# A planner's timeline model for the first half of a transformer layer, and a pool of its own for attention's queries and keys

## The chip, the cores and the metric

The kernel runs on one core of one Trainium2 chip. A core has a matrix engine (TensorE, PE in the profile, with its weight loads as PEld), a vector engine (VectorE, DVE), a scalar engine (ScalarE, ACT), a third elementwise engine (GpSimd, POOL) and SyncE (SP), which here only issues transfers. Each engine works through its own queue of instructions in order; semaphores make one engine wait for another. The metric is the device time of one execution in microseconds, as the median of several runs.

## The reference

One layer of an encoder on 1024 tokens of width 1024, in float32:

```
x = x + 1/2 * post1(SwiGLU_1(pre1(x)))                # first FFN, inner width 2816
u = pre_mix(x)
[ret_q|ret_k|ret_v|ret_g|na_q|na_k|na_v|g_ret|g_na] = u @ W_mix_in
y_ret = W_ret_out(silu(ret_g) * headnorm(retention forward + backward))   # 4 heads
y_na  = W_na_out(2-D neighbourhood attention(na_q, na_k, na_v) + bias)    # 8 heads
x = x + post_mix(W_mix_out(sigmoid(g_ret) * y_ret + sigmoid(g_na) * y_na))
x = x + 1/2 * post2(SwiGLU_2(pre2(x)))                # second FFN
```

pre, post and headnorm are RMS norms; ret_q and ret_k are rotated by position (rotary) before the retention.

## The kernel before

**Precision.** Each float32 operand is split into a high part and a low part (`split`, lines 60 and 61: ACT casts the high part, DVE, or POOL where told, subtracts it from the source for the low part). A product is three matmuls, high by high, low by high and high by low (`mm3`, lines 87 to 89). So a 128x512 piece of weights costs one transfer, one ACT cast, one DVE subtraction and then matmuls.

**Stages.** In order: the first norm and its transposes (`norm_T`, `flip`, line 126 on PE); the first FFN's input half (`ffn_in`, `Pairs.run`), its output half (`ffn_out`) with an epilogue that squares, scales and normalises (`Epilogue`: L525 on ACT, L526 on POOL, L97 the reciprocal root on POOL, L536 and L547 on DVE); the mixing pairs; attention (`na_cores`) and retention (`ret_cores`), with other projections filled in between; the mixing output; the second FFN.

**Pairs.** The wide projections use Winograd's form of a 2x2 block product with seven products in place of eight. One call of `Pairs.run` is one job: it loads two 128x1024 pieces (raw, tag `wraw`, 4 buffers), makes differences of them in place on DVE (L383, L384, L397, L408), splits them (tags `wh`, `wl`, 9 buffers each) and evicts the seven products from PSUM (L381 on ACT, L387 to L414 on DVE). The mixing stage has 14 jobs: four for attention's queries and keys, then four rotary jobs alternating with four silu jobs, then two sigmoid jobs. A rotary job calls `rotate` for each of its four parts (L866 to L869), on POOL and DVE in turn. The results (attention's queries `nq` and keys `nk`, the gates `sn`, and so on) are stored to memory by POOL's queue (`store`, line 67) and read back later.

**Order.** The kernel is written in program order, but the framework's scheduler orders the instructions of every queue when it plans the program: it keeps program order as a priority, simulates the engines with a model of their costs, and at each simulated moment queues the ready instruction of the highest priority. On the chip each queue then runs in that fixed order. Three devices steer it: `Filler` interleaves pieces of independent work (an n in FILL tuples is a number of such steps), `high_priority` lifts a few instructions, and `behind` or `issue_after` put one instruction after another.

**Where the halves meet.** After the last sigmoid job the pools of the first half are closed (`left.close()`), the pool `mix` is opened, and `na_cores` starts. It loads head pair 0's keys (`load(0)`, as a `wraw` tile) and queries (`qload(0)`, four transfers, L699), splits them (L60/L61 and L63/L64), then runs `fill(n0)`, 12 steps of the value projection of the retention (`vproj(wrv...)`: one step is one `mm3`, three matmuls; three steps use up one 128x512 piece of weights), and then the first scores (L744). PSUM has eight banks: six of tag `ps`, two of tag `pt`. All tiles of `na_cores` come from one pool, `na`, whose memory lies over that of the closed pools of the first half.

Of the kernel before, what the change touches and what calls it, by code (L numbers as in the profile page):

```python
# [26 lines left out]
RH = 4  # L27
NHP = 4

NA_FILL = (12, 2, 2)  # L30
RET_FILL = (14, 2, 2, 4, 2, 3, 0, 1, 2)
FLIP_FILL = (8, 8, 8, 8, 2)
NA_UNITS = ((0, 0, 0), (3, 1, 0), (1, 0, 1), (1, 0, 2), (4, 1, 1), (4, 1, 2), (2, 0, 3), (5, 1, 3))
# [651 lines left out]
    return lhs  # L685


def na_cores(c, pool, d, bias, fill, n0, n1, n2, side={}):


    nc = c.nc
# [1 line left out]

    def qload(hp):

        qraw[hp] = [pool.tile([P, S], F32, tag="qraw", name="qraw", bufs=2) for _ in range(2)]
        for e in range(2):
            for half in range(2):
                nc.sync.dma_start(qraw[hp][e][64 * half:64 * half + 64], d["nq"][hp][64 * e:64 * e + 64])  # L699

    def qsplit(hp, cb):

        qop[hp, cb] = []
        for e in range(2):
            q = [pool.tile([P, 16, 16], F32R, tag=f"q{e}{p}", name=f"q{p}", bufs=2) for p in "hl"]
            c.split(*q, qraw[hp][e].rearrange("p (r c) -> p r c", c=64)[:, :, 16 * cb:16 * cb + 16], scale=0.125)
            qop[hp, cb].append([p.rearrange("p r c -> p (r c)") for p in q])

    def load(hp):
        if hp == 0:  # L710
            kr = c.raw(d["nk"][hp])
        else:
            kr = pool.tile([P, S], F32, tag="kraw", name="kraw", bufs=1)
            nc.sync.dma_start(kr, d["nk"][hp])

        kop[hp] = [pool.tile([P, S], F32R, tag=f"k{e}", name=f"k{e}", bufs=2) for e in range(2)]
        for e in range(2):
            es, es_ = slice(64 * e, 64 * e + 64), slice(64 - 64 * e, 128 - 64 * e)
            for b in range(2):
# [310 lines left out]
def trunk_layer(ctx: ExitStack, tc, x, g1a, w1i, w1o, g1b, gma, wmt, wnv, wrv, logits, dtab, rope, bias,  # L1030
# [26 lines left out]
    def rows(a):  # L1057
        return lambda t: a[t * P:(t + 1) * P, :]
# [4 lines left out]
        return stack.enter_context(tc.tile_pool(name=name, bufs=1, side=side))  # L1063


    apool = pool(right, "a1", "right")
    early = pool(right, "early", "right")
    wx = Winograd(c, (apool,) * 3, early, (14,) * 7)
    with tc.tile_pool(name="norm1", bufs=1) as ep:
        g = ep.tile([P, D], F32, tag="gpre", name="gpre", bufs=1)  # L1070
        nc.sync.dma_start(g, g1a)
        for t in range(TT):
            xt = ep.tile([P, D], F32, tag="epx", name="epx", bufs=3)
            nc.sync.dma_start(xt, x[t * P:(t + 1) * P, :])
            f = c.norm_T(xt, g, t, ep, wx.put)()
            if f is not None:
                f()
        fin = Pairs(c, wx, [(w1i[i], w1i[FT + i]) for i in LeftFactors.order], 3, 3)
        fin.lead(lambda: early.tile([P, 512], F32, tag="lead", name="lead", bufs=6), on_pool=(3, 4, 5, 0))
    g0 = pool(left, "gl10")  # L1080
    with tc.tile_pool(name="fin1", bufs=1) as fp:
        fin.side = Filler(right_factors(c, fin, early, "lead", 6, w1o, wf[0], 35))
        ffn_in(c, fin, fp, LeftFactors(c, early, gl[0]))
    right.close()

    spool = pool(left, "s1")
    x0pool = pool(right, "x0", "right")
    x1_stack = ExitStack()
    x1pool = pool(x1_stack, "x1", "right")
    wx = Winograd(c, (x0pool, x1pool, spool), None, (4, 4, 2, 8, 8, 8, 8), d["a21"])  # L1090
    ep_stack, g_stack = ExitStack(), ExitStack()
    ep = pool(ep_stack, "ep1")
    g1 = pool(g_stack, "gl11")
    xt = [x1pool.tile([P, 4, 512], F32, tag="x", name="x", bufs=2) for _ in range(2)]
    xt += [spool.tile([P, 4, 512], F32, tag="x", name="x", bufs=8) for _ in range(2)]
    junk = spool.tile([P, 4, 512], F32, tag="x", name="junk", bufs=8)
    q = [p.tile([P, 4, 512], F32, tag="x", name="q", bufs=n) for p, n in ((ep, 2), (ep, 2), (spool, 8), (spool, 8))]
    ahead = {}
    fo = Epilogue(c, ep, g1b, gma, rows(x), rows(x1), wx.put)
    rest = ffn_out(c, xt, [junk[:, i] for i in range(4)], q, Blocks(c, (g0, g1, g1, g1), (1, 3)), w1o, wf[0], gl[0], fo,  # L1100
                   {n: (lambda j=j: ahead.update({j: c.load_w(wnv[j])})) for j, n in enumerate((65, 66, 73))})
    g_stack.close()
    wx.tmp = pool(g_stack, "cmb1")


    a21 = []

    def xh(t, k):

        return a21 if (t, k) == (1, 0) else wx.op(("a11", "a12", None, "a22")[2 * t + k])  # L1110

    def vproj(src, groups, done):

        for toks in groups:
            banks = {t: c.bank() for t in toks}
            for k in range(KT):
                if k % 2 == 0:
                    w = ahead.pop(k // 2) if k // 2 in ahead else c.load_w(src[k // 2])
                for t in toks:
                    tt = slice((t % 4) * P, (t % 4 + 1) * P)  # L1120
                    c.mm3(banks[t], [q[:, k % 4, tt] for q in xh(t // 4, k // 4)], w[k % 2], k == 0, k == KT - 1)
                    yield
            for t in toks:
                done(t, banks[t])

    evpool = []

    def ev():
        return evpool[0].tile([P, S], F32, tag="ev", name="ev", bufs=3)

    def done_nv(t, b):
        e = evpool[0].tile([P, 512], F32, tag="ev", name="ev", bufs=6 if len(evpool) == 1 else 4)
        nc.scalar.copy(e, b)
        c.store(d["nv"][2 * t:2 * t + 2].rearrange("r c d -> (r c) d"), e)

    def done_rv(j):
        def f(t, b):
            e = ev()
            nc.scalar.copy(e[:, :512], b)
            c.store(d["rv"][t][:, j * 512:(j + 1) * 512], e[:, :512])  # L1140
        return f


    jobs = [(16 + i, 20 + i, d["nq"][i], d["nk"][i], None) for i in range(NHP)]
    for i in range(RH):
        jobs += [(i, 4 + i, d["rq"][i], d["rk"][i], "rotary"),
                 (8 + 2 * i, 9 + 2 * i, d["rg"][2 * i], d["rg"][2 * i + 1], AF.Silu)]
    jobs += [(32 + 2 * i, 33 + 2 * i, d["sn"][2 * i], d["sn"][2 * i + 1], AF.Sigmoid) for i in range(2)]
    mx = Pairs(c, wx, [(wmt[j[0]], wmt[j[1]]) for j in jobs], 3)

    def first():
        yield from vproj(wnv, ((0, 1, 2, 3),), done_nv)
        yield from mx.leads()

    fill = Filler(first())
    evpool[:] = [wx.tmp, None]
    for f, k in zip(rest, FLIP_FILL):
        fill(k)
        f = f()
        if f is not None:  # L1160
            fill(FLIP_FILL[4])
            f()
    g_stack.close()
    ep_stack.close()
    with tc.tile_pool(name="pa", bufs=1) as pa:
        evpool[:] = [pa]
        fill.drain()
        turners = (nc.gpsimd, nc.vector, nc.gpsimd, nc.vector)

        def half():  # L1170
            return pa.tile([P, 512], F32, tag="ev", name="ev", bufs=6)

        tabs = [[pa.tile([P, 512], F32, tag="tab", name="tab", bufs=4) for _ in range(2)] for _ in range(2)]
        for h in range(2):
            for j in range(2):
                nc.sync.dma_start(tabs[h][j], rope[:, j, h * 512:(h + 1) * 512])

        for i, (_, _, f, g, fn) in enumerate(jobs):
            parts = {}

            def part(j):
                parts[j] = half()
                return parts[j]

            def done(j):
                h = j % 2
                if fn == "rotary":
                    rotate(turners[j], half(), parts[j], *tabs[h])
                elif fn is not None:
                    nc.scalar.activation(parts[j], parts[j], fn)  # L1190
                c.store((f, g)[j // 2][:, h * 512:(h + 1) * 512], parts[j])
            mx.run(i, part, done)
            if i == 2:
                x1pool = pool(x1_stack, "x1b", "right")
                a21[:] = [x1pool.tile([P, 4, 512], F32R, name=f"a21{q}") for q in "hl"]
                for k in range(2):
                    raw = c.raw(d["a21"][:, 2 * k:2 * k + 2].rearrange("p k t -> p (k t)"))
                    c.split(*[q[:, 2 * k:2 * k + 2].rearrange("p k t -> p (k t)") for q in a21], raw)
            if i == NHP - 1:
                for _ in vproj(wnv, ((4, 5, 6, 7),), done_nv):  # L1200
                    pass
                for cb in range(4):
                    nc.sync.dma_start(d["nvg"][cb].rearrange("t (r c) d -> (t r) c d", r=4),
                                      d["nv"][:, KEY_OFF[cb]:KEY_OFF[cb] + 32, :])
    left.close()

    m_stack, o_stack = ExitStack(), ExitStack()
    mix = pool(m_stack, "mix")
# [49 lines left out]

    fill = Filler(products())
    dec = []  # L1260
    with tc.tile_pool(name="na", bufs=1) as na:
        na_cores(c, na, d, bias, fill, *NA_FILL, {24: lambda: dec.append(Decays(c, mix, logits, dtab))})
    dec = dec[0]
    fill.until("rv")
    with tc.tile_pool(name="ret", bufs=1) as ret:
# [155 lines left out]
```

## Time and profile before

| | us |
|---|---|
| median of 3 runs | 2291.7 (2291.03 to 2295.29) |
| the profiled execution's own time | 2290.08 |
| its span, first to last instruction | 2288.3 |
| PE busy | 2215.6 |
| DVE busy | 1700.4 |
| ACT busy | 1002.6 |
| POOL busy | 577.6 |

The span leaves 1.8 us of the execution outside it. A row in order of time has its start in us, its duration in us, engine, line, operation and `output<-inputs`, a count, and in brackets how long the engine stood idle before it and what ended that. A row of a stretch has, for each engine, busy time and the number of instructions, then the clock that PE was granted (1.00 is full speed), the busy share of the DMA engines and GB/s. Matmuls overlap, so a busy PE isn't PE at its peak; the number of PE instructions in a stretch tells more.

### The profile page before, as it was taken

To read this page: it belongs to the slowest core of one execution; us is meant where nothing else is said; L and a number is where in the kernel's file an instruction comes from. 1 tells how busy PE (TensorE), PEld (TensorE's weight loads), DVE (VectorE), ACT (ScalarE), POOL (GpSimd) and SP (SyncE) were. 2 spreads that over 40 slices of the span, in tenths; PEclk is the share of its full clock that TensorE was granted. 3 is DMA by queue.
4 is the path that set the end of the run, shared out by engine and by line. 5 is a ranking of instruction groups with operands and counts; after the bars stand their busy time and mean duration, and the time that the engine had idled before them with its cause. 6 is when DMAs were issued, how large, how long until landed. Compare 5 with 4: busy or idle time off the path is not lost.

```text
span 2288.3 us, 30130 instructions
## 1 busy us (share of the span) xinstructions
PE 2215.6 (97%) x10288; PEld 1836.6 (80%) x10288; DVE 1700.4 (74%) x2939; ACT 1002.6 (44%) x2102; POOL 577.6 (25%) x749
## 2 busy tenths in 40 slices
PE   6999999999999999999999999999899999999998
PEld 5888888878777887777888888888688888887886
DVE  8897878755878766968885677646997787875576
ACT  6332222344554222248885675315643222234453
POOL 3143434210221133411101222101324343421022
PEclk9999999999999999999999999999999999999999
DMA  4355545586653542257655467766534556447664
GB/s 156 117 189 172 189 166 193 174 279 196 228 163 138 175 162 98 94 192 249 209 175 173 157 222 237 259 228 216 189 126 156 189 175 203 155 167 244 191 234 155
DMA packets 161882, 422.62 MB, mean 185 GB/s; under 512 B 19712, under 2 KB 47488, under 8 KB 161664
## 3 DMA queue, kind: packets, MB, share of 16 engines
q1 hardware_dynamic: 121248, 286.97, 38.8%
q0 software_dynamic: 40480, 133.72, 15.7%
q8 instruction: 81, 1.33, 0.2%
q14 instruction: 73, 0.60, 0.1%
HBM read 301.60 MB, written 123.21 MB: 186 GB/s over the span
## 4 chain that ended last, share of the span: by engine, by line
PE 85%; DVE 8%; issue 2%; ACT 1%; POOL 1%; DMA 1%; POOLq 0%; DVEq 0%; SPq 0%; ACTq 0%
PE ps L89 26%; PE ps L87 26%; PE ps L88 26%; PE pt L87 1%; PE pt L88 1%; PE pt L89 1%; DVE wl L61 1%; PE ps L744 1%; PE pt L763 1%; POOL rstd L97 1%; PE pt L126 1%; DVE x L536 1%; DVE tmp L117 1%; DVE t L384 0%; PE pt L966 0%
## 5 line engine op out<-in xcount | busy, mean ns | idle before, releaser
L61 DVE TENSOR_TENSOR wl<-wraw,wh 128x512 fp32r<-128x512 f32 x662 | 500.9, 777 | 93.6 <-ACT wh L60 91.8
L60 ACT CAST wh<-wraw 128x512 fp32r<-128x512 f32 x670 | 391.0, 618 | 233.4 <-PE ps L88 82.8
L87 PE MATMUL ps<-wh,gh 128*128 128x512 f32 x612 | 239.3, 394 | 5.1 <-ACT gh L60 2.2
L88 PE MATMUL ps<-wl,gh 128*128 128x512 f32 x612 | 239.1, 392 | 3.6 <-DVE wl L61 3.6
L61 DVE TENSOR_TENSOR gl<-graw,gh 128x512 fp32r<-128x512 f32 (+2 forms) x178 | 124.0, 698 | 155.1 <-ACT gh L60 155.1
L89 PE MATMUL ps<-wh,gl 128*128 128x512 f32 x612 | 238.4, 393 | 0.9 <-DVE gl L61 0.8
L60 ACT CAST gh<-graw 128x512 fp32r<-128x512 f32 (+2 forms) x178 | 106.7, 601 | 211.2 <-PE ps L88 84.1
L60 ACT CAST wh<-t 128x512 fp32r<-128x512 f32 x58 | 36.1, 622 | 238.6 <-DVE t L384 238.6
L87 PEld LDWEIGHTS ps<-wh,gh 128*128 128x128 f32 x612 | 115.6, 189 | 30.8 <-ACT gh L60 2.6
L88 PEld LDWEIGHTS ps<-wl,gh 128*128 128x128 f32 x612 | 115.4, 189 | 29.3 <-DVE wl L61 6.1
L89 PEld LDWEIGHTS ps<-wh,gl 128*128 128x128 f32 x612 | 115.5, 189 | 25.9 <-DVE gl L61 2.0
L526 POOL TENSOR_TENSOR q<-q,gain 128x512 f32<-128x512 f32 x30 | 46.1, 1554 | 336.6 <-ACT junk L525 241.1
L89 PE MATMUL ps<-a11h,wl 128*128 128x512 f32 x280 | 112.4, 401 | 12.0 <-DVE wl L61 12.0
L87 PE MATMUL ps<-a11h,wh 128*128 128x512 f32 x280 | 113.1, 404 | 1.8 <-ACT wh L60 1.2
L88 PE MATMUL ps<-a11l,wh 128*128 128x512 f32 x280 | 111.6, 399 | 0.0
L89 PE MATMUL ps<-a12h,wl 128*128 128x512 f32 x280 | 109.6, 391 | 1.3 <-DVE wl L61 1.3
L87 PE MATMUL ps<-a12h,wh 128*128 128x512 f32 x280 | 110.6, 395 | 0.1
L87 PE MATMUL ps<-a22h,wh 128*128 128x512 f32 x280 | 109.8, 392 | 0.0
L88 PE MATMUL ps<-a12l,wh 128*128 128x512 f32 x280 | 109.3, 390 | 0.0
L89 PE MATMUL ps<-a22h,wl 128*128 128x512 f32 x280 | 109.1, 390 | 0.0
L88 PE MATMUL ps<-a22l,wh 128*128 128x512 f32 x280 | 109.1, 390 | 0.0
L400 DVE TENSOR_TENSOR c<-ps,gt 128x512 f32<-128x512 f32 x44 | 30.4, 691 | 99.5 <-PE ps L89 99.1
(362 smaller groups left out, 5967.1 us busy)
## 6 DMA issues: line engine op xcount, KB each, us to landing
wraw<-in_dram SPq DMA_DIRECT2D x243, 512.0 KB, 4.4
g0s<-cmb POOLq DMA_DIRECT2D x44, 256.0 KB, 2.7
lead<-in_dram POOLq DMA_DIRECT2D x44, 256.0 KB, 3.8
graw<-g0s SPq DMA_DIRECT2D x44, 256.0 KB, 2.8
wq<-in_dram POOLq DMA_DIRECT2D x44, 256.0 KB, 3.9
g1s<-cmb POOLq DMA_DIRECT2D x44, 256.0 KB, 3.7
graw<-g1s SPq DMA_DIRECT2D x44, 256.0 KB, 2.7
bt<-in_dram SPq DMA_DIRECT2D x24, 384.0 KB, 4.1
```

The lines of the kernel that those rows point to most:

```text
L60: nc.scalar.copy(h, src)
L61: (eng or nc.vector).tensor_tensor(l, src, hf, ALU.subtract)
L87: mm(ps, a[0], b[0], start=start, stop=False, skip_group_check=more)
L88: mm(ps, a[0], b[1], start=False, stop=False, skip_group_check=more)
L89: mm(ps, a[1], b[0], start=False, stop=stop, skip_group_check=more)
L97: self.nc.gpsimd.tensor_tensor(r[:, :n], ms, self.mhalf[:, :n], ALU.pow)
L117: nc.vector.scalar_tensor_tensor(xn[:, bs], x[:, bs], r[:, 0:1], gain[:, bs], op0=ALU.mult, op1=ALU.mult)
L126: self.nc.tensor.transpose(pt[:, j * P:(j + 1) * P], h[:, j * P:(j + 1) * P], self.ident)
L400: self.last = self.read = tt(c21, p7, c12, ALU.add).ins
L526: (eng or c.nc.gpsimd).tensor_tensor(h if out is None else out, h, self.post[:, b * 512:(b + 1) * 512], ALU.mult)
L536: nc.vector.scalar_tensor_tensor(x[:, bs], h, r[:, 0:1], x[:, bs], op0=ALU.mult, op1=ALU.add)
L744: nc.tensor.matmul(bv, q[:, rg * P:(rg + 1) * P], k, start=n == 0, stop=n == 1)
```

## The change

Everything from the first norm to the last mixing pair is put into a block of its own, `tc.block(schedule_with_timeline_sim=True)`. Inside it the scheduler plans with its second, more detailed model of the engines (TimelineSim); the rest of the kernel is planned with the default (CoreSim). By the framework's description the default leaves out the fixed cost of GpSimd's elementwise instructions and the other has it. A block is scheduled as a unit: nothing from outside is queued among its instructions; what depends on it is issued behind it; a pool slot that is released in it is free again only once the whole block has completed, while a direct read of a tile written in it waits for that write alone.

The last lines of the block now load head pair 0's keys (`kr0`) and the first three 128x1024 pieces of the retention's value weights (`ahead`, split at once into six 128x512 pieces), which the code behind it used to load. The queries (`qraw`, `q`) and the split keys (`k`) come from a new pool `nq`, opened ahead of `na`; the other tiles stay in `na`. `NA_FILL` starts with 16 steps where it had 12. No arithmetic changes.

```diff
-NA_FILL = (12, 2, 2)
+NA_FILL = (16, 2, 2)
...
-def na_cores(c, pool, d, bias, fill, n0, n1, n2, side={}):
+def na_cores(c, qpool, pool, d, bias, fill, kr0, n0, n1, n2, side={}):
...
-        qraw[hp] = [pool.tile([P, S], F32, tag="qraw", name="qraw", bufs=2) for _ in range(2)]
+        qraw[hp] = [qpool.tile([P, S], F32, tag="qraw", name="qraw", bufs=2) for _ in range(2)]
...
-            q = [pool.tile([P, 16, 16], F32R, tag=f"q{e}{p}", name=f"q{p}", bufs=2) for p in "hl"]
+            q = [qpool.tile([P, 16, 16], F32R, tag=f"q{e}{p}", name=f"q{p}", bufs=2) for p in "hl"]
...
         if hp == 0:
-            kr = c.raw(d["nk"][hp])
+            kr = kr0
...
-        kop[hp] = [pool.tile([P, S], F32R, tag=f"k{e}", name=f"k{e}", bufs=2) for e in range(2)]
+        kop[hp] = [qpool.tile([P, S], F32R, tag=f"k{e}", name=f"k{e}", bufs=2) for e in range(2)]
...
-    apool = pool(right, "a1", "right")
-    early = pool(right, "early", "right")
+    with tc.block(schedule_with_timeline_sim=True):
+        apool = pool(right, "a1", "right")
+        early = pool(right, "early", "right")
...
+                if i == len(jobs) - 1:
+                    kr0 = c.raw(d["nk"][0])
+                    ahead.update({j: c.load_w(wrv[0][j]) for j in range(3)})
+        left.close()
...
-    with tc.tile_pool(name="na", bufs=1) as na:
-        na_cores(c, na, d, bias, fill, *NA_FILL, {24: lambda: dec.append(Decays(c, mix, logits, dtab))})
+    with tc.tile_pool(name="nq", bufs=1) as nq, tc.tile_pool(name="na", bufs=1) as na:
+        na_cores(c, nq, na, d, bias, fill, kr0, *NA_FILL, {24: lambda: dec.append(Decays(c, mix, logits, dtab))})
```

The lines in between only move one level in, into the block.

More of the change, by code (lines that the diff above doesn't have):

```diff
@@ L1076, in trunk_layer @@
             if f is not None:
+                fill(FLIP_FILL[4])
                 f()
[L1078 to L1141, printed above, removed]
@@ L1144, in trunk_layer @@
[L1144 to L1204, printed above, removed]
@@ L1205, in trunk_layer, with half, part, done @@
-    left.close()
+        g_stack.close()
+        ep_stack.close()
+        with tc.tile_pool(name="pa", bufs=1) as pa:
+            evpool[:] = [pa]
+            fill.drain()
+            turners = (nc.gpsimd, nc.vector, nc.gpsimd, nc.vector)
+            def half():
+                return pa.tile([P, 512], F32, tag="ev", name="ev", bufs=6)
+            tabs = [[pa.tile([P, 512], F32, tag="tab", name="tab", bufs=4) for _ in range(2)] for _ in range(2)]
+            for h in range(2):
+                for j in range(2):
+                    nc.sync.dma_start(tabs[h][j], rope[:, j, h * 512:(h + 1) * 512])
+            for i, (_, _, f, g, fn) in enumerate(jobs):
+                parts = {}
+                def part(j):
+                    parts[j] = half()
+                    return parts[j]
+                def done(j):
+                    h = j % 2
+                    if fn == "rotary":
+                        rotate(turners[j], half(), parts[j], *tabs[h])
+                    elif fn is not None:
+                        nc.scalar.activation(parts[j], parts[j], fn)
+                    c.store((f, g)[j // 2][:, h * 512:(h + 1) * 512], parts[j])
+                mx.run(i, part, done)
+                if i == 2:
+                    x1pool = pool(x1_stack, "x1b", "right")
+                    a21[:] = [x1pool.tile([P, 4, 512], F32R, name=f"a21{q}") for q in "hl"]
+                    for k in range(2):
+                        raw = c.raw(d["a21"][:, 2 * k:2 * k + 2].rearrange("p k t -> p (k t)"))
+                        c.split(*[q[:, 2 * k:2 * k + 2].rearrange("p k t -> p (k t)") for q in a21], raw)
+                if i == NHP - 1:
+                    for _ in vproj(wnv, ((4, 5, 6, 7),), done_nv):
+                        pass
+                    for cb in range(4):
+                        nc.sync.dma_start(d["nvg"][cb].rearrange("t (r c) d -> (t r) c d", r=4),
+                                          d["nv"][:, KEY_OFF[cb]:KEY_OFF[cb] + 32, :])
+                if i == len(jobs) - 1:
+                    kr0 = c.raw(d["nk"][0])
+                    ahead.update({j: c.load_w(wrv[0][j]) for j in range(3)})
```

85 lines of the change are left out of this document (77 added, 8 removed).

## The prediction

> **What bounds the kernel now.** I read the page first (shares, then the chain of waits), then the busy time and instruction counts in stretches of 50 us, then the instructions in order of time at each stretch that fell short.
>
> ```profile
> span 2288.3 us, 30130 instructions
> ...
> PE 2215.6 (97%) x10288; PEld 1836.6 (80%) x10288; DVE 1700.4 (74%) x2939; ACT 1002.6 (44%) x2102; POOL 577.6 (25%) x749
> ...
> PE 85%; DVE 8%; issue 2%; ACT 1%; POOL 1%; DMA 1%; POOLq 0%; DVEq 0%; SPq 0%; ACTq 0%
> ```
>
> The matrix engine sets the end: 97% busy, 85% of the chain. No matmul is added or removed, so the change can only move the few stretches in which PE stands still or runs at a lower clock. The next rows are from the table of 50 us stretches; the columns are PE busy, its instruction count, PEld, DVE, ACT, POOL, the granted clock, the DMA share and GB/s.
>
> ```profile
> 50.00:100.00 50.00, 45.52 (x194) 37.16 (x193) 39.37 (x65) 18.69 (x31) 1.29 (x2) 0.97 0.23 74
> 450.00:500.00 50.00, 47.81 (x204) 39.08 (x203) 28.20 (x40) 21.93 (x39) 8.64 (x10) 0.97 0.84 294
> 550.00:600.00 50.00, 50.00 (x222) 41.41 (x221) 36.16 (x52) 23.17 (x45) 6.53 (x4) 1.00 0.67 212
> 600.00:650.00 50.00, 46.10 (x213) 37.58 (x212) 41.89 (x66) 30.90 (x70) 15.97 (x16) 1.00 0.72 235
> 650.00:700.00 50.00, 47.24 (x212) 38.31 (x211) 35.81 (x60) 25.15 (x56) 13.36 (x14) 0.97 0.36 121
> 700.00:750.00 50.00, 45.01 (x195) 35.37 (x194) 42.15 (x69) 18.72 (x34) 5.76 (x10) 0.97 0.46 151
> 850.00:900.00 50.00, 44.87 (x189) 36.08 (x188) 38.72 (x56) 15.82 (x30) 16.74 (x18) 0.97 0.28 101
> 1000.00:1050.00 50.00, 43.64 (x208) 35.37 (x207) 31.03 (x70) 28.44 (x62) 5.27 (x8) 1.00 0.78 250
> ```
>
> A full stretch, 550 to 600, holds 222 instructions: 50/222 = 0.225 us each. The six short stretches between 50 and 900 lack 28 + 18 + 9 + 10 + 27 + 33 = 125 of them, 28 us in all. That is the most that a better order of the first block could win back; slices that stand at 222 cannot win anything. The last row is the seam between the two halves, at 1015 us, where the new block ends.
>
> **Part one, the order of the first block.** Removed: nothing. Moved: potentially each instruction on each queue up to 1015 us, SP's loads and POOL's stores among them. What differs is the planner's idea of POOL: its default leaves out the fixed cost of POOL's elementwise instructions, the timeline model has it. So I look at the two stages where POOL does such work beside a short PE stretch.
>
> The four rotary jobs of the mixing pairs are the same work, so they compare with each other. Four stretches of 30 us, one round each job's rotation:
>
> ```profile
> 820.00:850.00 30.00, 29.18 (x128) 23.48 (x127) 25.87 (x31) 5.46 (x10) 15.08 (x13) 1.00 0.51 175
> 856.00:886.00 30.00, 24.87 (x101) 19.47 (x100) 21.57 (x27) 5.88 (x12) 14.04 (x13) 0.94 0.25 88
> 905.00:935.00 30.00, 29.18 (x127) 23.49 (x127) 25.80 (x31) 5.40 (x10) 15.13 (x13) 1.00 0.19 68
> 944.00:974.00 30.00, 29.19 (x128) 23.52 (x127) 25.66 (x31) 5.16 (x9) 15.20 (x14) 1.00 0.26 96
> ```
>
> Three of them run 127 or 128 PE instructions, the second 101. In time order, first the DVE in the first job, then ACT, DVE and PE in the second:
>
> ```profile
> 824.48 0.69 DVE L400 TENSOR_TENSOR ev<-ps,ev 128x512 f32<-128x512 f32 x1 [2.03 <-PE ps L89]
> 825.09 0.68 DVE L383 TENSOR_TENSOR wraw<-wraw 128x512 f32<-128x512 f32 x1
> ...
> 857.41 0.62 ACT L60 CAST wh<-wraw 128x512 fp32r<-128x512 f32 x1
> ...
> 864.01 0.69 DVE L400 TENSOR_TENSOR ev<-ps,ev 128x512 f32<-128x512 f32 x1 [2.03 <-PE ps L89]
> ...
> 875.67 1.75 DVE L61 TENSOR_TENSOR wl<-wraw,wh 128x512 fp32r<-128x512 f32 x1
> 877.45 1.64 DVE L383 TENSOR_TENSOR wraw<-wraw 128x512 f32<-128x512 f32 x1
> ...
> 877.47 0.79 PE L89 MATMUL ps<-a11h,wl 128*128 128x512 f32 x1 [4.89 <-DVE wl L61]
> ```
>
> In the first job the difference for the next job (L383) is queued directly behind the eviction of L400. In the second, evictions and rotation steps are queued ahead of L383 and of the low part wl (L61), though ACT's last cast of a high part was done 18 us before and DVE had idled 2.03 us ahead of L400. That is an accident of the planned order, not of the data. If the new order brings this job to its sisters, it wins 128 - 101 = 27 instructions, 27 x 0.225 = 6.1 us. Bounds: 0 (the accident returns) to 6.1. I take 6.1, as three of four jobs are rows of the good case.
>
> The other stage is the epilogue of the first FFN. Its two PE stalls, and POOL and DVE before them:
>
> ```profile
> 608.90 3.00 POOL L526 TENSOR_TENSOR q<-q,gain 128x512 f32<-128x512 f32 x2 [15.44 <-ACT ps L525]
> 611.86 0.56 POOL L97 TENSOR_TENSOR rstd<-ss,mhalf 128x1 f32<-128x1 f32 x1
> 619.39 0.63 PE L126 MATMUL ps<-ident,q 128*128 128x128 f32 x4 [2.21 <-ACT wh L60]
> ...
> 678.93 2.44 DVE L536 SCALAR_TENSOR_TENSOR x<-q,rstd,x 128x512 f32<-128x512 f32 x2 [0.43 <-POOL rstd L97]
> 681.08 1.44 POOL L526 TENSOR_TENSOR q<-q,gain 128x512 f32<-128x512 f32 x1
> 681.41 2.32 DVE L536 SCALAR_TENSOR_TENSOR x<-q,rstd,x 128x512 f32<-128x512 f32 x2
> 685.79 1.12 PE L126 MATMUL pt<-ident,q 128*128 128x128 f32 x5 [2.76 <-DVE q L547]
> 686.35 2.73 DVE L536 SCALAR_TENSOR_TENSOR x<-q,rstd,x 128x512 f32<-128x512 f32 x4
> ...
> 686.10:689.40 3.30, 3.30 (x12) 2.78 (x11) 3.11 (x7) 2.40 (x7) 1.70 (x3) 0.50 0.36 135
> ```
>
> At 608.90 two multiplications of 1.5 us each stand on POOL ahead of the 0.56 us rstd that the first tile waits for, and PE, whose queue was planned as if they cost little, stops at its transposes for 2.21 us while other matmuls of that FFN are behind them. With the right cost the transposes are planned later, and that stall goes: 2.2 us, bounds 0 to 2.2. At 678.93 two pairs of L536 take 4.76 us where four in a row take 2.73 at 686.35: 2.0 us are lost to POOL's L526 beside them. Moving those off that chain leaves a stall of 0.7 us. The last row shows what else goes: after the 2.76 us stall the granted clock is 0.50 over 3.3 us, which costs half of it, 1.65 us. Together 2.0 + 1.65 = 3.7 us, bounds 0 to 3.7. I take both, 5.9 us: POOL's cost is what the two planners disagree on, and both chains pass through it.
>
> [...] The trace has a lower clock after a stall of 2.76 us. [...]
>
> The stretches 50 to 100 (DVE 39.37 of 50 us busy on the first norm's factors) and 450 to 500 (a round trip of the FFN's factors through memory) I cost at nothing: there DVE's work or a DMA is the limit in any order. Bounds: 0 to 28 x 0.225 + 18 x 0.225 = 10.4 us; a new order could also lose as much in such places as the second rotary job loses now, 6.1 us. Sum of part one: 6.1 + 5.9 = 12.0 us won.
>
> **Part two, the end of the block.** A slot released in the block (a PSUM bank, a piece of wh, the memory of the closed pools) is free again only when the whole block is complete, its last store included. Today the work behind the last pair flows into it:
>
> ```profile
> 1015.35 0.39 PE L89 MATMUL ps<-s4h,wl 128*128 128x512 f32 x1
> 1015.58 0.39 PE L87 MATMUL ps<-wh,a11h 128*128 128x512 f32 x1
> ...
> 1017.43 0.54 POOL L67 DMA_DIRECT2D sn<-ev  x1 [2.18 <-ACT ev L1190]
> ...
> 1021.10 2.30 ACT L60 CAST k<-wraw 64x512 fp32r<-64x512 f32 x4 [0.58 <-DMA sn<-ev]
> 1021.09 2.41 SPq L699 DMA_DIRECT2D qraw<-nq  x4
> ...
> 1027.47 0.72 ACT L63 ACTIVATE qh<-qraw 128x256 fp32r<-128x256 f32 x2 [2.90 <-DMA qraw<-nq]
> ...
> 1027.99 0.42 PE L744 MATMUL ps<-k,qh 128*128 128x384 f32 x1 [1.82 <-issue]
> ```
>
> The last pair's matmul ends at 1015.35 + 0.39 = 1015.74; PE goes straight on with the value projection (wh, a11h). The last store lands about 1021.10, when ACT and SP are let go. If PE's next bank has to wait for that, PE stands 1021.10 - 1015.74 = 5.4 us, and by the 2.76 us stall above a stretch of half clock follows, 1.65 us. Queued behind that first matmul are the sixteen filling steps, then the scores. Bounds: 0 (PE waits only for its own bank, as now) to 7.0 us. I take the upper end: nothing that PE does next writes to memory that the block never used.
>
> The loads moved into the block (nk, three of wrv: 512 KB each) are on SP before its end; their six pieces are what PE needs first, so no load is added to the stall. Sixteen steps are 48 matmuls x 0.225 = 10.8 us, against 8.1 us for twelve. Queries still come 1027.99 - 1021.10 = 6.9 us after the block ends, so 10.8 us cover them: the 1.82 us of waiting at 1027.99 go. Bounds: 0 to 1.8; I take 1.8. The pool of its own (nq) could let queries load before the last store, up to 5.4 us earlier; the memory under it is also freed in the block, so I cost it at 0. It would be hidden by the sixteen steps anyway. The four added steps are taken from later ones. Sum of part two: 7.0 - 1.8 = 5.2 us lost.
>
> **Sum.** 12.0 - 5.2 = 6.8 us won, from the profiled execution's own 2290.08 us: 2283.3. That execution stands 1.6 us below the median of the runs (2291.7), so the forecast is 2285 us, 0.3% less. A change under 0.2%, 4.6 us, can't be told from none here.
>
> **Rivals.** *The block's end decides (slower).* Place: PE's first bank behind the last store. Price: 5.2 us net, 7.0 if the queries come late too. It decides from the point where the order wins less than 0.6 us, since 5.2 - 0.6 = 4.6. For it: from 600 to 650 us DVE's 41.89 and POOL's 15.97 us make 57.9 of 50, and the wl at 875.67 took 1.75 us, so a new order may only move the waits. Time: 2291.7 + 5.2 to 7.0, say 2298. Against it: the sister jobs above.
>
> [...]
>
> *The greedy order turns against the epilogue (no change).* All L526 come before the rstd in program order. A planner that knows their 1.5 us finds them ready first and may put all four, 6.0 us, ahead of the rstd: 3.0 us later than now. The 2.2 us are not won and 3.0 + 1.65 lost: 12.0 - 2.2 - 4.7 - 5.2 = 0, 2292 us. For it: at 611.86 the rstd slipped in after two, which a costlier model may not allow.
>
> *The block's end is cheap (faster).* PE waits for its bank alone; part two is -1.8 us: 12.0 + 1.8 = 13.8 won, 2278 us. Against it: today ACT and SP, which do wait for the freed memory, wait until 1021.1.
>
> *The change doesn't do what it says*: the two models agree on these orders. Then part two alone is left, which is the first rival's time.
>
> **How the numbers follow.** Forecast 0.42, block's end with nothing won 0.24, greedy order 0.17, cheap end 0.17. The forecast's own range is 2279 to 2290 (each of its terms at half); about 0.32 of its 0.42 lie below 2287.1, 0.10 within 0.2%. So faster 0.32 + 0.17 = 0.49; same 0.10 + 0.17 = 0.27; slower 0.24. The 8-in-10 range reaches from the cheap end with some of the 10.4 us, 2273, to the block's end with a little lost order, 2300.
>
> **What would show it.** Right: 127 or 128 PE instructions in all four rotary stretches, no clock of 0.97 between 600 and 700 us, a PE gap of about 5 us where the pairs end, released by a DMA, and none at the first scores. Wrong: full PE between the last pair and the value projection (part two was too dear), or a new PE stall above 3 us inside FFN or pairs (the order lost what it should win).

## The result, and the profile after

The kernel after takes 2279.36 us (median of 6 runs, 2277.84 to 2281.71), the kernel before beside it 2293.49 us (6 runs, 2291.03 to 2296.91). The ratio is 0.9939, 95% interval 0.9926 to 0.9951: 14 us faster, twice the 6.7 us forecast and inside the range. The profiled execution took 2278.68 us with a span of 2276.6 us.

The page of the kernel after, its span, busy time by engine and chain of waits by engine:

```profile
span 2276.6 us, 30177 instructions
...
PE 2213.0 (97%) x10288; PEld 1839.2 (81%) x10288; DVE 1694.7 (74%) x2939; ACT 1001.8 (44%) x2102; POOL 592.2 (26%) x749
...
PE 43%; issue 7%; DVE 4%; DMA 2%; POOL 2%; ACT 1%; SPq 0%; POOLq 0%; DVEq 0%; ACTq 0%
```

The work is the same: 10288 matmuls. The chain's shares are no measure of the change: they add up to 59% here and to 98% before, so here the chain is only partly followed back.

The table of stretches of the kernel after answers to the one in the prediction (PE busy, its instruction count, PEld, DVE, ACT, POOL, granted clock, DMA share, GB/s). All lie some microseconds further on in the work than the stretches of the same name before:

```profile
50.00:100.00 50.00, 49.22 (x220) 40.25 (x219) 42.40 (x69) 20.11 (x34) 5.23 (x7) 1.00 0.25 79
450.00:500.00 50.00, 45.50 (x196) 36.06 (x195) 26.98 (x38) 21.98 (x39) 8.19 (x10) 1.00 0.83 289
600.00:650.00 50.00, 50.00 (x235) 41.66 (x234) 45.23 (x70) 32.14 (x73) 20.89 (x16) 1.00 0.70 218
650.00:700.00 50.00, 50.00 (x234) 41.59 (x233) 38.70 (x66) 26.17 (x58) 18.73 (x17) 1.00 0.49 168
700.00:750.00 50.00, 40.03 (x175) 32.03 (x174) 41.13 (x66) 17.77 (x30) 4.16 (x7) 0.90 0.36 117
850.00:900.00 50.00, 50.00 (x222) 41.42 (x221) 43.73 (x57) 15.23 (x28) 24.15 (x23) 1.00 0.37 120
1000.00:1050.00 50.00, 43.70 (x222) 37.38 (x221) 37.39 (x98) 34.69 (x84) 4.26 (x5) 0.93 0.84 271
```

PE is now full from 600 to 700 and from 850 to 900 us. Between 700 and 750 it is worse than before (175 instructions against 195), and 450 to 500 is not better.

A clearer reading is the time at which PE begins a named instruction, in one profiled execution of each kernel. The last two columns are each kernel's own distances: from the first to the last s4 product, which is the length of the mixing pairs, and from the last s4 product to the last score.

| kernel | first product of the FFN's output | first s4 product of the pairs | last s4 product | first score | last score | pairs | end of pairs to last score |
|---|---|---|---|---|---|---|---|
| before | 455.2 | 742.7 | 1015.4 | 1028.0 | 1193.2 | 272.7 | 177.8 |
| after | 451.8 | 736.0 | 996.9 | 1008.4 | 1179.0 | 260.9 | 182.1 |
| block, default model | 455.2 | 742.9 | 1015.5 | 1027.0 | 1198.5 | 272.6 | 183.0 |
| timeline model alone | 451.9 | 736.2 | 997.1 | 1024.4 | 1185.3 | 260.9 | 188.2 |
| parts at the end alone | 454.9 | 742.3 | 1014.9 | 1026.0 | 1192.5 | 272.6 | 177.6 |
| after, no early loads | 452.5 | 736.9 | 997.8 | 1022.9 | 1183.9 | 260.9 | 186.1 |
| after, no pool of its own | 452.4 | 737.5 | 998.4 | 1010.0 | 1179.6 | 260.9 | 181.2 |
| timeline model for all | 452.3 | 738.1 | 999.0 | 1010.1 | 1200.5 | 260.9 | 201.6 |

So 18.5 us are won up to the last pair: 3.4 ahead of the FFN's output, 3.3 through it and its epilogue, 11.8 in the pairs. The way to the last score gives back 182.1 - 177.8 = 4.3. That makes 14.2 up to the last score. The rest, from the last score to the end, takes 1095.1 us in the one profile and 1097.6 in the other; over all the kernels below but the one planned wholly by the timeline model it varies from 1094.7 to 1101.5 us. So the two profiled executions differ by 11.4 us in all, and that 14.2 lies so near the 14.1 us of the medians is partly chance.

**Pairs.** The four rotary jobs after, in stretches of 30 us that each hold one job's rotation:

```profile
801.00:831.00 30.00, 30.00 (x134) 24.82 (x134) 15.84 (x21) 8.14 (x14) 9.16 (x10) 1.00 0.65 219
837.00:867.00 30.00, 30.00 (x135) 24.82 (x133) 26.77 (x38) 9.90 (x19) 11.59 (x13) 1.00 0.37 126
886.00:916.00 30.00, 30.00 (x134) 24.82 (x134) 26.68 (x32) 7.72 (x14) 14.43 (x12) 1.00 0.35 104
925.00:955.00 30.00, 30.00 (x134) 24.83 (x133) 26.50 (x32) 7.26 (x14) 15.00 (x13) 1.00 0.33 105
```

All hold 134 or 135 instructions; the three good ones before held 127 or 128. DVE in the second rotary job after, in order of time:

```profile
855.87 0.69 DVE L400 TENSOR_TENSOR ev<-ps,ev 128x512 f32<-128x512 f32 x1 [2.03 <-PE ps L89]
856.47 0.68 DVE L383 TENSOR_TENSOR wraw<-wraw 128x512 f32<-128x512 f32 x1
857.19 1.66 DVE L384 TENSOR_TENSOR t<-wraw 128x512 f32<-128x512 f32 x1
```

The next job's difference (L383) is directly behind the eviction (L400), as in the first job before. The next row (L384) takes 1.66 us where it takes 0.69 at 843.07 and 880.86, and PE has no gap in this stretch (30.00 of 30.00 us busy): the order has made room.

**Epilogue.** POOL at the first rstd, then the end of the epilogue on PE and ACT, in order of time in the kernel after:

```profile
607.41 1.30 POOL L526 TENSOR_TENSOR q<-q,gain 128x512 f32<-128x512 f32 x1 [12.48 <-ACT ps L525]
608.67 0.56 POOL L97 TENSOR_TENSOR rstd<-ss,mhalf 128x1 f32<-128x1 f32 x1
609.24 5.01 POOL L526 TENSOR_TENSOR q<-q,gain 128x512 f32<-128x512 f32 x3
...
714.24 0.66 PE L126 MATMUL pt<-ident,q 128*128 128x128 f32 x4 [1.92 <-ACT cmb L272]
721.49 0.62 ACT L60 CAST s2h<-cmb 128x512 fp32r<-128x512 f32 x1 [0.59 <-DVE cmb L284]
722.16 0.80 PE L87 MATMUL ps<-s2h,wh 128*128 128x512 f32 x1 [7.27 <-ACT s2h L60]
```

The stretch over that end, as in the tables above:

```profile
715.00:725.40 10.40, 3.24 (x7) 2.32 (x8) 9.56 (x16) 4.54 (x8) 0.19 (x1) 0.51 0.37 126
```

The rstd now follows one L526, not two. PE has no stall above 0.25 us between 600 and 712 us, where before it had 2.21, 1.61 and 2.76 us. But work was only moved forward. The value projection of attention, which used to cover the epilogue's end, now runs from 668.07 to 693.69 us, before from 677.43 to 708.42; its first result is copied out at 691.60, before at 707.46. So PE reaches the last transposes with nothing left to do, stands 1.92 and 7.27 us, and has a clock of 0.51 over that end, while DVE (9.56 of 10.40 us busy) makes the last factors.

**The block's end.** The same rows of each engine, after:

```profile
996.88 0.39 PE L89 MATMUL ps<-s4h,wl 128*128 128x512 f32 x1
997.11 0.39 PE L87 MATMUL ps<-wh,a11h 128*128 128x512 f32 x1
...
997.30 2.41 SPq L699 DMA_DIRECT2D qraw<-nq  x4
998.95 0.54 POOL L67 DMA_DIRECT2D sn<-ev  x1 [2.18 <-ACT ev L1191]
1004.58 0.34 SPq L734 DMA_DIRECT2D bt<-in_dram  x1
1004.97 0.42 SPq L71 DMA_DIRECT2D wraw<-in_dram  x1
...
1009.03 1.14 ACT L60 CAST wh<-wraw 128x512 fp32r<-128x512 f32 x2 [3.22 <-DMA wraw<-in_dram]
1012.86 2.42 ACT L60 CAST wh<-wraw 128x512 fp32r<-128x512 f32 x4 [0.56 <-DMA wraw<-in_dram]
1013.51 1.97 DVE L61 TENSOR_TENSOR wl<-wraw,wh 128x512 fp32r<-128x512 f32 x3 [0.48 <-ACT wh L60]
1015.39 0.55 DVE L745 CUSTOM_DVE_ANT_0 s<-ps,bt 128x384 f32<-128x384 f32 x1
...
1016.01 0.69 PE L744 MATMUL ps<-k,qh 128*128 128x384 f32 x1 [3.61 <-DVE nast L745]
1022.10 0.30 PE L763 MATMUL pt<-ident,s 128*128 128x128 f32 x1 [2.70 <-issue]
```

PE goes from the last pair (996.88) to the value projection (997.11) at full pace, and the queries' load (997.30) starts before the last store is even issued (998.95). Two stalls come later instead, 3.61 and 2.70 us. The bias table's load waits until 1004.58; the profile puts 4.5 us of that down to the landing of the last store, so it waits for freed memory. The next weights stand behind it on SP and are cast at 1009.03 and 1012.86. On DVE three of their low parts (1013.51) are queued ahead of the eviction of the first scores (L745, 1015.39), and for that eviction PE stands 3.61 us.

### The profile page after: what moved, and what is told of

Read it like the earlier page. It is cut to its first block, busy times and chain, and to the rows that moved or that the text cites. A ratio compares the mean times of both kernels' runs of the same rounds, so it can differ in the third digit from the quotient of the medians.

```text
span 2276.6 us, 30177 instructions
## 1 busy us (share of the span) xinstructions
PE 2213.0 (97%) x10288; PEld 1839.2 (81%) x10288; DVE 1694.7 (74%) x2939; ACT 1001.8 (44%) x2102; POOL 592.2 (26%) x749
## 4 chain that ended last, share of the span: by engine, by line
PE 43%; issue 7%; DVE 4%; DMA 2%; POOL 2%; ACT 1%; SPq 0%; POOLq 0%; DVEq 0%; ACTq 0%
PE ps L87 13%; PE ps L89 13%; PE ps L88 13%; DVE wl L61 1%; PE pt L89 1%; PE pt L87 1%; PE pt L88 1%; DMA wraw<-in_dram 0%; POOL rstd L97 0%; PE pt L966 0%; DVE x L536 0%; ACT wh L60 0%; DMA vraw<-nvg 0%; DMA sn<-ev 0%; PE pt L914 0%
## 5 line engine op out<-in xcount | busy, mean ns | idle before, releaser
L61 DVE TENSOR_TENSOR wl<-wraw,wh 128x512 fp32r<-128x512 f32 x662 | 482.3, 751 | 90.7 <-ACT wh L60 88.5
L526 POOL TENSOR_TENSOR q<-q,gain 128x512 f32<-128x512 f32 x30 | 52.9, 1780 | 333.7 <-ACT junk L525 121.5
L400 DVE TENSOR_TENSOR c<-ps,gt 128x512 f32<-128x512 f32 x44 | 30.4, 691 | 104.4 <-PE ps L89 104.2
```

What stands on the lines that cost most here:

```text
L61: (eng or nc.vector).tensor_tensor(l, src, hf, ALU.subtract)
L400: self.last = self.read = tt(c21, p7, c12, ALU.add).ins
L526: (eng or c.nc.gpsimd).tensor_tensor(h if out is None else out, h, self.post[:, b * 512:(b + 1) * 512], ALU.mult)
```

## The experiments

The theory after the result: the order that the timeline model gives wins the 18.5 us. Rival one: the parts at the block's end make the gain. Rival two: it is a lucky order, not a better model.

**The block with the default model.**

```
-    with tc.block(schedule_with_timeline_sim=True):
+    with tc.block():
```

> The block stays, with the loads, the pool and the sixteen steps, but it is planned by the default model. Theory (the timeline model's order wins, 18.5 us up to the last pair): the 12 to 18 us are lost again, 2290 to 2297 us, and the rotary job or the epilogue shows its stalls again. Rival one (the block itself, or the parts at its end, make the gain): 2278 to 2282 us. A time between, 2283 to 2288, would divide the gain between the two.

Measured: 2297.26 us, ratio 1.0011 (0.9998 to 1.0023), at the upper end of the theory's range. The whole gain is gone, and the stall of the second rotary job is back; PE in this kernel:

```profile
877.63 0.80 PE L89 MATMUL ps<-a11h,wl 128*128 128x512 f32 x1 [4.90 <-DVE wl L61]
```

Every time up to the last pair is that of the kernel before within 0.2 us (third row of the table). So the model, not the block, makes the gain. The block has a price: the kernel without it but with the same parts, below, has the ratio 0.9986 (0.9975 to 0.9996), and from the end of the pairs to the last score it takes 177.6 us against 183.0. Those two distances come from one profiled execution each, and the runs of each of the two kernels spread over some 7 us.

**The timeline model alone.**

```
     with tc.block(schedule_with_timeline_sim=True):
...
-                    kr0 = c.raw(d["nk"][0])
-                    ahead.update({j: c.load_w(wrv[0][j]) for j in range(3)})
...
-NA_FILL = (16, 2, 2)
+NA_FILL = (12, 2, 2)
...
-        na_cores(c, nq, na, d, bias, fill, kr0, *NA_FILL, ...)
+        na_cores(c, na, na, d, bias, fill, *NA_FILL, ...)
```

> The block with the timeline model, but none of the parts at its end: no early loads of nk and wrv, queries and keys in the old pool, twelve filling steps. Theory (order): the last pair still ends 18 to 19 us earlier than before; the attention starts worse by 2 to 7 us, so 2281 to 2287 us. Rival one (parts at the end make the gain): 2291 to 2295 us.

Measured: 2284.62 us, ratio 0.9960 (0.9947 to 0.9974). Of the 14 us, 9 come with the model alone; up to the last pair it is the kernel after. Against that kernel it loses time in one place, behind the last pair. SP, ACT and PE there:

```profile
997.13 0.39 PE L89 MATMUL ps<-s4h,wl 128*128 128x512 f32 x1
...
1002.25 0.49 SPq L699 DMA_DIRECT2D qraw<-nq  x1
1005.20 1.06 SPq L71 DMA_DIRECT2D wraw<-in_dram  x2
1012.34 2.35 ACT L60 CAST wh<-wraw 128x512 fp32r<-128x512 f32 x4 [0.42 <-DMA wraw<-in_dram]
1013.01 0.79 PE L87 MATMUL ps<-wh,a11h 128*128 128x512 f32 x1 [15.49 <-ACT wh L60]
```

PE stands 15.49 us. The weights' loads come behind the queries' on SP, and the first of those goes only at 1002.25; the first weight is asked for at 1005.20 and cast at 1012.34.

**The parts at the end alone.**

```
-    with tc.block(schedule_with_timeline_sim=True):
+    if True:
```

> No block at all: the early loads, the pool of its own and the sixteen steps in the kernel before. Theory (order): the stalls up to 1015 us stay, at most the 1.82 us wait at the first scores goes: 2289 to 2294 us. Rival one (parts at the end make the gain): 2279 to 2283 us.

Measured: 2290.58 us, ratio 0.9986 (0.9975 to 0.9996): 3 us. Without a block's end they are worth little; rival one is out.

**The timeline model for the whole kernel.**

```
-    with tc.block(schedule_with_timeline_sim=True):
+    if True:
...
-    with tile.TileContext(nc) as tc:
+    with tile.TileContext(nc, schedule_with_timeline_sim=True) as tc:
```

> No block; the timeline model plans the whole kernel, with the parts at the end kept. Theory (the model knows POOL's cost, so it wins wherever POOL stands in a chain): the first half as in the kernel after, the second half the same or better, 2268 to 2280 us. Rival two (a lucky order in the first half only, no better model): the second half may lose as much as the first won, 2282 to 2305 us.

Measured: 2318.39 us, ratio 1.0111 (1.0090 to 1.0131): slower than either range, in the direction of rival two. Its pairs are as good as after (260.9 us), its attention is the worst of all. The stretch of attention in this kernel, then in the kernel after:

```profile
1000.00:1200.00 200.00, 179.54 (x982) 155.76 (x981) 154.70 (x452) 147.88 (x375) 20.02 (x27) 0.97 0.64 202
```

```profile
1000.00:1200.00 200.00, 193.24 (x1087) 168.15 (x1086) 161.60 (x474) 156.71 (x403) 19.36 (x27) 0.98 0.69 218
```

PE executes 982 instructions there against 1087. From the last score to the end this kernel takes 1118.1 us, where all others take at most 1101.5. So the model is no better in general: here it wins 16.4 us up to the last pair (1015.4 and 999.0 in the table) and loses more in the second half. That the change stops it at the pairs' end is what makes it pay.

**No pool of its own.**

```
-    with tc.tile_pool(name="nq", bufs=1) as nq, tc.tile_pool(name="na", bufs=1) as na:
-        na_cores(c, nq, na, d, bias, fill, kr0, ...)
+    with tc.tile_pool(name="na", bufs=1) as na:
+        na_cores(c, na, na, d, bias, fill, kr0, ...)
```

> The kernel after, with queries and keys back in attention's one pool. Theory (a pool opened in that place waits for the memory of the last store, as the first bias table does at 1004.58 in the kernel after, 7.3 us behind the queries): queries are ready only some 11.5 us after 1000, the sixteen steps end at 1008.4, so PE stands 3 to 6 us at the first scores: 2280 to 2285 us. Rival (the steps hide it): no gap, 2278 to 2281 us.

Measured: 2275.63 us, ratio 0.9921 (0.9906 to 0.9935). This is below both ranges. The theory's first step came true: the queries are asked for at 1004.01, 5.6 us behind the start of the last s4 product, where the kernel after asks 0.4 us behind it. But PE waits only 1.11 us at the first scores, and the 3.61 us stall is not there; one of 2.67 us at 1020.70 is left. The interval overlaps that of the kernel after, so the pool is worth nothing that these runs can tell.

**No early loads.**

```
-            kr = kr0
+            kr = c.raw(d["nk"][hp])
...
-                if i == len(jobs) - 1:
-                    kr0 = c.raw(d["nk"][0])
-                    ahead.update({j: c.load_w(wrv[0][j]) for j in range(3)})
```

> The kernel after, but nk and the three weights are loaded behind the block. Theory (the 15.49 us stall seen with the model alone is the wait for the first weight of the value projection, and the early loads are what take it away): PE stands 10 to 16 us behind the last pair, released by a cast of wh, 2283 to 2290 us. Rival (the pool of its own or the sixteen steps take it away): no stall above 4 us there, 2278 to 2282 us.

Measured: 2284.85 us, ratio 0.9959 (0.9945 to 0.9973). SP, ACT and PE in this kernel:

```profile
1001.21 1.66 SPq L71 DMA_DIRECT2D wraw<-in_dram  x3
1009.07 3.20 ACT L60 CAST wh<-wraw 128x512 fp32r<-128x512 f32 x6
1009.73 0.79 PE L87 MATMUL ps<-wh,a11h 128*128 128x512 f32 x1 [11.54 <-ACT wh L60]
```

The stall is back with 11.54 us. Of the parts at the end it is the early loads that matter; they are worth some 5 us of the total, since part of the 11.54 us is made up in attention (second and sixth rows of the table: 182.1 and 186.1 us). The pool and the sixteen steps, which this kernel has and the timeline model alone has not, make no difference that shows: 2284.85 and 2284.62 us.

**Is it POOL's cost?** The rotation on DVE alone, in the kernel before and in the kernel after:

```
-            turners = (nc.gpsimd, nc.vector, nc.gpsimd, nc.vector)
+            turners = (nc.vector,) * 4
```

> The kernel before, with the rotation on DVE alone instead of half of it on POOL, so POOL has no elementwise work left in the mixing pairs. To be read beside the same edit in the kernel after. Before this edit the stretch from the first to the last s4 product of the pairs is 272.7 us before and 260.9 us after. Theory (the two models disagree over POOL's cost): the two kernels now come within 4 us of each other in that stretch. Rival (the orders differ for another reason): the difference stays between 8 and 14 us.

> The kernel after, with the rotation on DVE alone. Theory (POOL's cost): its pairs' stretch is within 4 us of that of the kernel before with the same edit. Rival (another reason): 8 to 14 us shorter.

Measured, in one execution of each: 2301.97 and 2275.61 us. The pairs take 273.5 us in the one and 260.9 us in the other; the difference is 12.6 us, not under 4. DVE and PE in the second rotary job of the first of the two:

```profile
864.14 0.68 DVE L400 TENSOR_TENSOR ev<-ps,ev 128x512 f32<-128x512 f32 x1
...
877.71 0.69 DVE L61 TENSOR_TENSOR wl<-wraw,wh 128x512 fp32r<-128x512 f32 x1
...
878.45 0.80 PE L89 MATMUL ps<-a11h,wl 128*128 128x512 f32 x1 [5.77 <-DVE wl L61]
```

With no elementwise work of POOL in the pairs, the default model still puts evictions and rotation ahead of wl, and PE still stands 5.77 us. So POOL's cost in the pairs is not why the two models differ there. POOL's elementwise work ahead of the pairs, in the epilogue, was left in place, so it is not shown that its cost plays no part at all. What in the default model puts the second job's steps so late was not found.

**Four at attention's start.** The kernel after again; with twelve steps; with a fourth weight asked for behind the block and the bias tables in the queries' pool; and without the pool of its own but with the fourth weight:

```
-NA_FILL = (16, 2, 2)
+NA_FILL = (12, 2, 2)
...
+    ahead[3] = c.load_w(wrv[0][3])
     fill = Filler(products())
...
-            bts[hp, var] = pool.tile([P, 2, 384], ...)
+            bts[hp, var] = qpool.tile([P, 2, 384], ...)
```

> The kernel after, unchanged, beside three of its relatives. If leaving out the pool of its own was really worth 2 to 4 us (2275.6 against 2279.4 us in separate sets), this one comes at 2278 to 2281 us again; if that was only the difference between two sets, at 2275 to 2277 us.

> The kernel after with twelve filling steps ahead of the scores. Theory (the prediction's: the four added steps cover the queries' way, 1.8 us): the steps end 2.7 us earlier, at 1005.7, the queries' casts at 1005.8 to 1006.3, so at most 1 us of waiting appears there, and the four steps are there for the 3.61 us stall at 1012.4: 2277 to 2281 us. Rival (sixteen are needed): PE stands 2 us or more at the first scores: 2281 to 2285 us.

> The kernel after with a fourth weight of wrv asked for behind the block, and the bias tables in the queries' pool. Theory (the 3.61 us stall at 1012.4 is a chain: the bias table's load waits for freed memory until 1004.58, the next weight's load stands behind it on SP, its low part ahead of the scores' eviction on DVE): that stall goes with its half clock, 3 to 5 us: 2273 to 2277 us. Rival (attention's start is bound by DVE or by the landing of other loads anyway): a new wait of 2 to 4 us near 1010 to 1022: 2278 to 2281 us.

> The kernel without the pool of its own, with a fourth weight of wrv asked for behind the block. Theory (the same chain): 2 to 3 us below the kernel without the pool alone (2275.6 us), 2272 to 2275 us. Rival (with queries and bias tables both let go only by the last store, the first scores decide): no change, 2275 to 2278 us.

Measured, in this order: 2277.90, 2277.96, 2275.76 and 2275.82 us; ratios 0.9930 (0.9916 to 0.9944), 0.9923 (0.9909 to 0.9936), 0.9920 and 0.9920 (both 0.9906 to 0.9934). None is told apart from another. The first lies between its two ranges, the second and third lie in those of their theories, the fourth in that of its rival. The first scores' stalls, with twelve steps and then with the fourth weight and the bias tables moved:

```profile
1015.97 0.69 PE L744 MATMUL ps<-k,qh 128*128 128x384 f32 x1 [5.13 <-DVE nast L745]
```

```profile
1015.37 0.45 PE L744 MATMUL ps<-k,qh 128*128 128x384 f32 x1 [1.93 <-DVE nast L745]
1021.87 0.45 PE L763 MATMUL pt<-ident,s 128*128 128x128 f32 x1 [4.49 <-issue]
```

With four steps fewer the scores begin 2.7 us sooner behind the pairs, but the stall behind the first of them grows to 5.13 us; moving the loads shortens it to 1.93 but makes the next one 4.49, as that run's rival had it. Whatever is moved, the way from the end of the pairs to the last score took 180.5 to 184.1 us in these four; without a block's end it took 177.6. No variant clearly beats the kernel after.

## Why the prediction came out as it did

**Part one, 12.0 us forecast, 18.5 measured.** This is the step that was mis-sized. *The second rotary job*: its place and mechanism were right (127 or more instructions in all four stretches was the sign named), but the 6.1 us were counted against its sister jobs, as if those were full. They were not: 30 us hold 134, as the prediction's own 0.225 us each would have told (30 / 0.225 = 133). The four stretches of 30 us lacked 53 instructions together, 53 x 0.225 = 11.9 us. The whole of the pairs as one stretch, before and then after:

```profile
742.70:1015.70 273.00, 265.43 (x1154) 216.69 (x1153) 199.23 (x276) 81.48 (x142) 79.36 (x89) 0.99 0.39 138
```

```profile
736.00:997.30 261.30, 261.30 (x1154) 216.39 (x1153) 201.34 (x274) 79.64 (x138) 80.00 (x89) 1.00 0.41 138
```

The same 1154 instructions take 273.0 and 261.3 us: 11.7, the sisters' losses included. DVE and POOL are as busy as before; what is gone is 7.6 us of PE's waiting and the lower clock (0.99 against 1.00). *The epilogue*: 5.9 us forecast. The two stalls named went, and a third (1.61 us at 646.85); but 1.92 and 7.27 us, and a clock of 0.51 behind them, came at its end, so FFN output and epilogue together won 3.3. The prediction did not ask what would be late once the stalls were gone: it was DVE, with the last factors. Its ceiling of 28 us was too low as well: full stretches between 600 and 700 hold 235 and 234 instructions, not 222, for the transposes there (L126) are shorter: the eight that begin at 620.08 take 1.03 us together, 0.13 each against 0.225. *The stretch 50 to 100*, costed at nothing because DVE was held to be the limit in any order, went from 194 to 220 instructions; with 13 fewer in the 50 us ahead of it (141 against 154), that leaves 13, 2.9 us, most of the 3.4 us won ahead of the FFN's output. *The reason*, POOL's cost, fell for the pairs. In the epilogue the rstd did move ahead of the second L526, as that reason would have it, but no experiment tried it there: for the 3.3 us of that stage the reason stays open.

**Part two, 5.2 us lost forecast, 4.3 measured, in another place.** The step that failed is PE's wait for its bank: PE did not stand 5.4 us behind the last pair, nor at all. ACT's and SP's wait of before, on which it rested, was one for memory (in a pool of their own the queries do not wait: their load goes at 997.30), and PE's banks were not held so: its next product started at 997.11, before the last store was issued. By the description of a block ahead of the prediction, a bank released in it would have been held; these runs do not show that. What was costed at nothing, the early loads, is what PE's next work hung on: without them it stands 11.54 us. The loss came at the scores instead (3.61 and 2.70 us, with a clock of 0.55 over the 3.4 us behind the first), where no wait had been forecast. That 4.3 lies so near 5.2 is therefore luck. The pool of its own at 0 us was right in the sum and wrong in the reason: the queries' load does start before the last store. The 1.8 us of waiting at the first score did go, but not by the sixteen steps: with twelve it is gone too.

**The signs and the range.** Of the signs of being right, 127 or more instructions in all rotary stretches, no clock of 0.97 between 600 and 700 us and no wait at the first score came; the PE gap of about 5 us did not. Both signs of being wrong came: full PE between the last pair and the value projection, and a new stall above 3 us (7.27) where the epilogue ends and the pairs begin. The forecast's own range of 2279 to 2290 does not follow from "each of its terms at half": that gives about 2281 (only the 7.0 halved) to 2291 (only part one halved). The measured 2279.36 lies below that; it is inside the 8-in-10 range.

**The rivals.** The cheap end (2278) came nearest, and by its mechanism at the pairs' end; it left out the loss in attention and the larger part one. The slower first rival fell with both of its terms. DVE's and POOL's 57.9 us of work in the 50 from 600 us on, and the wl of 1.75 us, stood for it, as signs that a new order may only move the waits. In the pairs the two rotation runs speak against that: they gain 12.6 us with POOL's elementwise work taken out and 11.8 with it in, so what the order won there does not hang on POOL's work beside DVE. The greedy order did not come: one L526 stands ahead of the first rstd, not four. Later in the epilogue, ahead of the rstd at 675.71, there are two, where before there was one.

## What to carry to other kernels

A stage that seems sound beside its sisters is to be measured against a full stretch of the same instruction, or the common loss of all sisters is left out. Where a block ends, ask first which load the matrix engine's next operand needs and what stands ahead of it on the issuing queue; asking for it inside the block took a stall of 11.5 us away, some 5 us of the total. A planner's model that wins in one half of a kernel can lose more in the other, so it is tried by stages.

## What was not expected of the hardware

A stall of the same length (2.19 us) at the same place was followed by a clock of 0.57 in one execution and of 1.00 in another. At the start of the FFN's output, the stall in the order of time and then the stretch of some 3.4 us behind it, first in the kernel before:

```profile
460.23 0.50 PE L87 MATMUL ps<-wh,gh 128*128 128x512 f32 x1 [2.19 <-ACT gh L60]
```

```profile
460.23:463.60 3.37, 3.37 (x9) 2.65 (x10) 3.37 (x3) 1.50 (x3) 3.33 (x5) 0.57 0.96 349
```

and the same two in the kernel after:

```profile
456.87 0.50 PE L87 MATMUL ps<-wh,gh 128*128 128x512 f32 x1 [2.19 <-ACT gh L60]
```

```profile
456.87:460.30 3.43, 2.98 (x12) 2.12 (x13) 3.43 (x2) 2.03 (x4) 3.39 (x5) 1.00 1.04 337
```

Both stalls are 2.19 us; the clock is 0.57 behind the one and 1.00 behind the other. In the kernel before, the clock is 0.50 from 460.72 to 464.14, for 3.42 us, and 1.00 on either side; an estimate from that is 1.7 us lost. The order on PE behind the stall is not the same in these two kernels, but it doesn't decide: of the ten profiles here in which the timeline model planned the first FFN, six have a clock of 1.00 over the 3.4 us behind this stall (1.99 to 3.12 us long) and four have 0.52 to 0.65. The four with the default model's order have 0.57 to 0.66. So profiles of one kernel can differ by some microseconds. The two of the kernel after stand 11.2 and 14.2 us below the kernel before at the last score; from 712 to 737 us the clock is 0.73 in the first and 0.80 in the second, from 997 to 1030 us 0.84 and 0.90. Their stalls at the scores differ too (4.28 and 3.61 us), so the clock is not shown to be the whole of it. What decides whether the clock falls behind such a stall is not shown.
